# A list-scheduled two-block transformer kernel: a margin for ScalarE's and VectorE's results in the plan, scores over 128 rows, constants asked for later

## The chip, the cores and the metric

The kernel runs on one core of a Trainium2 chip. The metric is device time in microseconds of one execution; each kernel is run several times and the median is given. A profiled execution is a separate run, with its own time and its own span from the first to the last instruction.

## What is computed

Two transformer blocks follow each other on one sequence of 256 tokens of width 1024, all in fp32. The first block is a gated feed-forward layer, a mixer, and a second gated feed-forward layer. Its mixer projects to a pooling branch (four sliding means) and to attention with 8 query heads of width 64 over 2 key/value heads, a window of 128 and a learned sink per head. Cut to the part that the change touches:

```python
def swa_with_sinks(q, k, v, sinks):              # 8 query heads, 2 kv heads, G = 4, 2 blocks of 128
    s = jnp.einsum('bnqkgd,bnjkd->bnkgqj', qb, kb) * (HEAD_DIM ** -0.5)
    s = jnp.where(valid, s, NEG_INF)             # a band of 128 keys
    p = jax.nn.softmax(jnp.concatenate([s, sink], axis=-1), axis=-1)[..., :-1]
    return jnp.einsum('bnkgqj,bnjkd->bnqkgd', p, vb)
```

The second block has a mixer of its own (a state-space branch with 16 heads and a latent attention with 16 heads), attention over 256 memory tokens, and a feed-forward layer with a short convolution.

## The kernel before

Tokens stand in two tiles t = 0, 1 of 128. Every weight matrix comes from HBM once, in blocks of 128x1024 fp32. ScalarE rounds a block to fp32r (`hi`), VectorE takes the rest (`lo = raw - hi`), and TensorE forms three products, hi·hi, hi·lo and lo·hi (`mm3`, `mm2`, `projB`). So each weight block costs a cast on ScalarE, a subtraction on VectorE and 12 to 24 matmuls. Nearly all the rest (softmax, norms, convolutions, gates) runs on VectorE and ScalarE between matmuls.

**The order is planned.** `K`'s methods don't issue anything: every call records a node in `Plan` (`add`), with its estimated duration (`cost`, line 293) and its dependences. `Plan.schedule` (line 339) is a list scheduler. It keeps a clock per engine and takes, over and over, the recorded instruction that can start first by its plan; ties go to the one recorded first. An instruction is ready when the results it reads are there, and a result counts as there only a fixed time after its end, by the table `HOP` (line 206), from the producing engine to the reading one:

```python
for u in n.users:
    u.ready = max(u.ready, n.end + max(HOP[e][x] for x in u.alts))
```

The plan's times decide nothing but order: `issue` (line 501) emits the instructions in order of planned start, each engine then runs its own queue in order, and semaphores make it wait for what isn't there yet. Because all instructions are issued from one line, every row of the profile is at L514 and every tile is called `t`.

Where TensorE would have to wait in the plan, the scheduler fills in other ready matmuls, as far as buffers allow: 8 PSUM banks, a fixed number of SBUF slots of each size, and limits on how far ahead a buffer may be taken (`SLOTS`, `RESERVE`, `AHEAD`). `mixer2` is written in the order of `STEPS` (line 33), where steps of the latent attention (`mla_proj`, `mla_attn`), of the state-space branch (`ssd_x`, `ssd_z`, `ssd_rec`), of the output projection and of the memory keys take turns.

**Scores in `mixer1`** (line 1026). The query tile is transposed in pairs: column block i of `qT[t]` holds head i (of kv group 0) in partitions 0 to 63 and head 4+i (of kv group 1) in partitions 64 to 127. `kT` holds the two kv heads one over the other in the same way. A score is one fp32 matmul per head and key block, over the 64 partitions of its head, added onto a mask that bf16 matmuls put into the bank first. There are 8 of them for t = 0 and 16 for t = 1, in groups of one PSUM bank (4 or 2 heads).

**Constants.** `ffn` for the first feed-forward layer calls `side(f0)` (line 1679) from its loop over column blocks f0 = 2, 4, ..., 20; at f0 = 4, 6, 8 and 10 it asks for the constants `cst` and `cols`, builds the rotary tables and builds constants of the state-space branch. At f0 = 8 the gain `ffn1_post` is asked for (line 929). All these transfers are on the same queue (SP) as the weights, in the order that the plan gives.

Of the kernel before, what the change touches and what calls it, by code (L numbers as in the profile page):

```python
# [18 lines left out]
P = 128  # L19
# [180 lines left out]
class Node:  # L200
# [4 lines left out]

HOP = {
    "PE": {"PE": 0.0, "ACT": 200.0, "DVE": 200.0, "POOL": 240.0, "SP": 240.0},
    "ACT": {"PE": 155.0, "ACT": 140.0, "DVE": 133.0, "POOL": 180.0, "SP": 180.0},
    "DVE": {"PE": 140.0, "ACT": 118.0, "DVE": 125.0, "POOL": 166.0, "SP": 166.0},
    "POOL": {"PE": 55.0, "ACT": 33.0, "DVE": 33.0, "POOL": 40.0, "SP": 55.0},  # L210
    "SP": {"PE": 50.0, "ACT": 30.0, "DVE": 30.0, "POOL": 30.0, "SP": 0.0},
}
# [12 lines left out]
class Plan:  # L225
# [66 lines left out]
    @staticmethod  # L292
    def cost(attr, op, a, k):
        out = k.get("out", a[0] if a else None)
        size = lambda v: int(np.prod(v.shape[1:]))
        ps = any(isinstance(v, View) and v.tile.cls == "ps" for v in list(a) + list(k.values()))
        if attr == "tensor":
            if op == "transpose":
                return 109.0
            n, dt = size(out), k["rhs"].dtype  # L300
            if dt == F32R:
                return 4.0 + (0.4453 * n if n >= 256 else 4 * n / 2.4)
            return 2 * max(4 + 0.8906 * n, 109.0) if dt == F32 else 4 + 0.4453 * n
        if op == "dma_start":
            return max(int(np.prod(out.shape)) * 4 / 395.0, 300.0)
        if attr == "scalar":
            scalars = sum(isinstance(v, View) for v in (k.get("scale"), k.get("bias"), a[2] if op == "mul" else None))
            return 0.833 * size(out) + (58 if ps else 94) + 88 * scalars + (98 if "accum_out" in k else 0)
        if attr == "vector":
            if op == "reduce_max":  # L310
                return 1.04 * size(a[1]) + 70
            one = op in ("tensor_copy", "tensor_scalar") and not ps
            scalars = op in ("tensor_scalar", "scalar_tensor_tensor") and any(isinstance(v, View) for v in (a[2], a[3] if op == "tensor_scalar" else None))
            return (0.52 if one else 1.04) * size(out) + 70 + 60 * scalars
        return 550.0 if size(out) == 1 else 1.05 * size(out) + 464

    def loud(self, n):
# [299 lines left out]
class K:  # L617
# [276 lines left out]
    def ffn(self, name, src, nxt, side=None, first=None):  # L894
# [21 lines left out]
        for f0 in range(0, KF, 2) if first else (0, *range(4, KF, 2)):  # L916
# [9 lines left out]
                held = f0, [(f, evac_at[0][f], evac_at[1][f]) for f in range(2)]  # L926
                continue
            w = [self.wblocks(w_gu, KD, o + f0 * P, o + (f0 + n) * P) for o in (0, DFF)]
            if f0 == 8:
                post = self.bc(self.w1024(), a[name + "_post"][0])  # L930
            if side:
                side(f0)
# [93 lines left out]
    def mixer1(self, xT, nxt):  # L1026
        nc, a = self.nc, self.a
        self.phase = "mix"
        sink = self.rows[:, :8]
        nsink = self.const("nsink", [P, 8])  # L1030
        nc.vector.tensor_scalar(nsink, sink, -1.0, None, op0=ALU.mult)
        mask = self.const("mask", [P, 256], BF16)
        nc.vector.tensor_copy(mask, self.cst[:, C_SWA : C_SWA + 256])
# [12 lines left out]
        psc = self.bc(pw[:, 512:], a["pool_scale"][0])  # L1046
        post = self.bc(self.w1024(), a["mix_post"][0])
        kvs, us, qTs = self.w1024(), self.w1024(), self.w1024()
        u, v, kT, qT, y = [], [], [], [], []
        for t in range(2):  # L1050
            self.label(f"mix1 win t{t}")
            x, r = xT[t]
            qk = self.w1024()[:, :640]
            pk, pq = self.tps(), self.tps()
            for k in range(KD):
                self.mm3(pk[:, :256], x, k, wkv[k], k == 0, k == KD - 1)
            for k in range(KD):
                self.mm3(pq, x, k, wq[k], k == 0, k == KD - 1)
            self.label(f"mix1 qk t{t}")
            vt = kvs[:, 2 * t * P : (2 * t + 1) * P]  # L1060
            nc.vector.tensor_scalar(vt, pk[:, P:256], r, None, op0=ALU.mult)
            nc.vector.tensor_scalar(qk[:, 512:], pk[:, :P], r, 0.125, op0=ALU.mult, op1=ALU.mult)
            nc.scalar.mul(qk[:, :512].rearrange("p (i j c) -> p j i c", j=2, c=64),
                          pq.rearrange("p (j i c) -> p j i c", j=2, c=64), r)
            v.append(vt)
            self.apply_rope(qk.rearrange("p (h c) -> p h c", c=64)[:, :, :16], t, 0, 8)
            tp = self.tps()
            nc.tensor.transpose(tp[:, :P], qk[:, 512:640], self.ident)
            kt = kvs[:, (2 * t + 1) * P : (2 * t + 2) * P]
            self.copy(kt, tp[:, :P])  # L1070
            kT.append(kt)
            tp = self.tps()
            for i in range(4):
                nc.tensor.transpose(tp[:, i * P : (i + 1) * P], qk[:, i * P : (i + 1) * P], self.ident)
            qt = qTs[:, t * 512 : (t + 1) * 512]
            self.copy(qt, tp)
            qT.append(qt)

            self.label(f"mix1 u t{t}")
            pu = self.tps()  # L1080
            for k in range(KD):
                self.mm3(pu, x, k, wu[k], k == 0, k == KD - 1)
            ut = us[:, t * 512 : (t + 1) * 512]
            self.scale(ut, pu, r)
            u.append(ut)
            y.append(self.w1024())
# [4 lines left out]
        for t in range(2):  # L1091
# [8 lines left out]
            for h0 in range(0, 8, nh):  # L1100
                sc = self.tps()
                for j in range(nh):
                    nc.tensor.matmul(sc[:, j * W : (j + 1) * W], lhsT=idb, rhs=mask[:, 256 - W : 256], start=j == 0, stop=False)
                for j in range(nh):
                    g, i = (h0 + j) // 4, (h0 + j) % 4
                    for kb in range(nk):
                        o = j * W + kb * P
                        nc.tensor.matmul(sc[:, o : o + P], lhsT=qT[t][64 * g : 64 * g + 64, i * P : (i + 1) * P],
                                         rhs=kT[t - nk + 1 + kb][64 * g : 64 * g + 64, :], start=False,
                                         stop=j == nh - 1 and kb == nk - 1)  # L1110
                pT, rd = self.softmax_p(sc, nh, W, (sink[:, h0 : h0 + nh], nsink[:, h0 : h0 + nh]))
                po = self.tps()
                for j in range(nh):
                    g = (h0 + j) // 4
                    for kb in range(nk):
                        o = j * W + kb * P
                        nc.tensor.matmul(po[:, j * 64 : (j + 1) * 64], lhsT=pT[:, o : o + P],
                                         rhs=v[t - nk + 1 + kb][:, 64 * g : 64 * g + 64], start=kb == 0, stop=kb == nk - 1)
                o = 512 + 64 * h0
                nc.vector.tensor_tensor(  # L1120
                    y[t][:, o : o + 64 * nh].rearrange("p (h c) -> p h c", c=64),
                    po[:, : 64 * nh].rearrange("p (h c) -> p h c", c=64),
                    rd.unsqueeze(2).to_broadcast([P, nh, 64]), op=ALU.mult)


            self.label(f"mix1 pool t{t}")
# [538 lines left out]
def trace(k, nc, a, out):  # L1665
# [11 lines left out]
            nx.done(t)  # L1677

    def side(f0):
        if f0 == 4:  # L1680
            nc.sync.dma_start(k.cst, a["cst"])
        if f0 == 6:
            nc.sync.dma_start(k.cols, a["cols"])
            k.bc(k.rows, a["rows"][0])
        if f0 == 8:
            k.rope_tables()
        if f0 == 10:
            k.ssd_constants()

    for name, how, part in (  # L1690
# [32 lines left out]
```

## Time and profile before

| | |
|---|---|
| median of 3 runs | 983.09 us (982.91 to 983.23) |
| the profiled execution's own time | 983.15 us |
| its span, first to last instruction | 981.4 us |
| TensorE (PE) busy | 967.9 us, 6474 matmul records |
| weight loads (PEld) busy | 877.8 us |
| VectorE (DVE) busy | 704.0 us |
| ScalarE (ACT) busy | 522.6 us |
| granted TensorE clock | 0.999 over the span |

Times inside the span are counted from its first instruction. An fp32 matmul leaves two records, an fp32r or bf16 matmul and a transpose leave one. A matmul's record lasts from its start to a modelled end, and the next one starts before that end; PE is therefore shown as busy also where it issues more slowly than it could, and an idle time of PE is only what lies behind a modelled end. PEld waits are the times for which a weight load stood still, whether or not a matmul was still running beside it.

### The profile page before, as it was taken

Reading aid. Unit: us, or ns where it says so; the run is one execution under the profiler, and the core shown is the slowest. Engines: PE = TensorE matmul, PEld = TensorE weight load, DVE = VectorE, ACT = ScalarE, POOL = GpSimd, SP = SyncE. Lnnn points to the kernel's source line nnn. Section 1 sums busy time; section 2 is a strip of 40 time slices with the busy share of each in tenths; the row PEclk is TensorE's granted clock in tenths of the full one; section 3 lists DMA queues with packets and bytes.
Section 4 is the critical chain, followed back from the end, with each engine's and each line's share of the span. In section 5 each row is a group of like instructions: output and inputs, shape, how many; then the busy total and the mean of one; then the engine's idle time right before and its main releaser. Section 6 shows DMA issues by size and latency. Waiting matters only on the chain.

```text
span 981.4 us, 16455 instructions
## 1 busy us (share of the span) xinstructions
PE 967.9 (99%) x6474; PEld 877.8 (89%) x6474; DVE 704.0 (72%) x1185; ACT 522.6 (53%) x866; POOL 40.4 (4%) x53
## 2 busy tenths in 40 slices
PE   9999999999999999999999999999999999999997
PEld 8999988887889999888998988888898899999887
DVE  6985544667596556447998799997866699897543
ACT  6853424546565333245777777454555476645341
POOL 0000000310010000000200000000000010000000
PEclk9999999999999999999999999999999999999999
DMA  9985545663247555454554336045654456518411
GB/s 322 384 278 173 155 150 171 209 224 116 95 157 280 183 166 159 142 156 145 170 171 152 128 114 250 23 131 181 226 173 141 152 171 231 195 58 299 133 62 43
DMA packets 50286, 168.54 MB, mean 172 GB/s; under 512 B 5792, under 2 KB 8352, under 8 KB 50208
## 3 DMA queue, kind: packets, MB, share of 16 engines
q1 hardware_dynamic: 49920, 166.96, 51.7%
q8 instruction: 51, 0.84, 0.4%
q10 hardware_dynamic: 288, 0.52, 0.1%
q14 instruction: 27, 0.22, 0.1%
HBM read 166.42 MB, written 1.05 MB: 171 GB/s over the span
## 4 chain that ended last, share of the span: by engine, by line
PE 83%; DVE 9%; ACT 3%; DMA 2%; issue 2%; POOL 1%; SPq 0%; POOLq 0%; ACTq 0%; DVEq 0%
PE t L514 83%; DVE t L514 9%; ACT t L514 3%; DMA t<-in_ffn_w_gu_from_dram 2%; POOL t L514 1%; DMA t<-in_xT_dram 0%; ACT L514 0%; SPq L514 0%; POOLq L1719 0%; ACTq L514 0%; DVEq L514 0%; POOLq L514 0%
## 5 line engine op out<-in xcount | busy, mean ns | idle before, releaser
L514 PE MATMUL t<-t,t 128*128 128x256 f32 (+5 forms) x6466 | 964.7, 312 | 5.9 <-DVE t L514 3.4
L514 PEld LDWEIGHTS t<-t,t 128*128 128x128 f32 (+3 forms) x6450 | 875.9, 186 | 93.6 <-DVE t L514 9.4
L514 DVE TENSOR_TENSOR t<-t,t 128x1024 fp32r<-128x1024 f32 (+9 forms) x756 | 572.3, 802 | 208.3 <-PE t L514 128.1
L514 ACT CAST t<-t 128x1024 fp32r<-128x1024 f32 (+6 forms) x400 | 350.9, 908 | 224.9 <-PE t L514 190.9
L514 ACT ACTIVATE t<-t 128x512 f32<-128x512 f32 (+8 forms) x133 | 73.7, 556 | 154.4 <-DVE t L514 121.8
L514 ACT ACTIVATE t<-t,t 128x256 f32<-128x256 f32 (+5 forms) x150 | 74.3, 525 | 52.1 <-PE t L514 35.6
L514 DVE SCALAR_TENSOR_TENSOR t<-t,t,t 128x255 f32<-128x255 f32 (+5 forms) x169 | 75.3, 499 | 24.9 <-ACT t L514 21.5
L514 POOL TENSOR_TENSOR t<-t,t 128x1 f32<-128x1 f32 x38 | 36.5, 962 | 835.5 <-DVE t L514 835.4
L514 ACT COPY t<-t 128x256 f32<-128x256 f32 (+3 forms) x51 | 21.8, 446 | 18.7 <-PE t L514 18.5
L514 DVE CAST t<-t 128x512 fp32r<-128x512 f32 (+8 forms) x54 | 21.2, 395 | 7.7 <-PE t L514 4.8
L514 DVE TENSOR_REDUCE t<-t 128x1 f32<-128x125 f32 (+2 forms) x38 | 19.5, 514 | 3.5 <-PE t L514 3.5
L514 DVE SCALAR_TENSOR_TENSOR t<-t,t 128x512 f32<-128x512 f32 (+4 forms) x34 | 12.6, 378 | 10.1 <-ACT t L514 9.8
L514 DVE TENSOR_SCALAR t<-t,t 128x128 f32<-128x128 f32 (+6 forms) x31 | 9.5, 318 | 9.0 <-PE t L514 4.6
L514 ACT ACTIVATION_READ_ACCUMULATOR t<-t 128x1 f32 x61 | 11.6, 191 | 0.0
L514 ACT ACT_TABLE_LOAD x7 | 9.0, 1283 | 3.0 <-DVE t L514 2.2
L514 ACT ACTIVATION_READ_ACCUMULATOR t<-t,t 128x1 f32 x48 | 10.6, 220 | 0.0
L514 DVE TENSOR_SCALAR t<-t 128x1 f32<-128x1 f32 (+6 forms) x44 | 6.2, 166 | 4.2 <-DMA t<-in_xT_dram 2.2
L514 DVE COPY t<-t 128x512 f32<-128x512 f32 (+6 forms) x14 | 5.4, 386 | 0.6 <-PE t L514 0.6
L514 DVE SCALAR_TENSOR_TENSOR t<-t 128x1 f32<-128x1 f32 (+1 forms) x17 | 2.6, 156 | 4.3 <-ACT t L514 4.1
L514 ACT ACTIVATE t<-t,t,t 128x256 f32<-128x256 f32 x8 | 4.5, 562 | 2.1 <-DVE t L514 2.1
L514 PEld LDWEIGHTS <-t 128*128 128x128 bf16 x24 | 2.3, 114 | 3.5 <-issue 1.9
L514 POOL MEMSET t<- 128x128 f32 x5 | 1.0, 204 | 95.9 <-PE t L514 91.4
(10 smaller groups left out, 12.8 us busy)
## 6 DMA issues: line engine op xcount, KB each, us to landing
t<-in_ffn_w_gu_from_dram SPq DMA_DIRECT2D x84, 512.0 KB, 5.8
t<-in_ffn_w_down_from_dram SPq DMA_DIRECT2D x44, 512.0 KB, 3.9
t<-in_w_ffn_up_from_dram SPq DMA_DIRECT2D x44, 512.0 KB, 4.7
t<-in_w_in_from_dram SPq DMA_DIRECT2D x34, 512.0 KB, 4.8
t<-in_w_out_from_dram SPq DMA_DIRECT2D x24, 512.0 KB, 4.8
t<-in_w_ffn_down_from_dram SPq DMA_DIRECT2D x22, 512.0 KB, 5.3
t<-in_w_mem_k_from_dram SPq DMA_DIRECT2D x8, 512.0 KB, 6.7
t<-in_w_mem_q_from_dram SPq DMA_DIRECT2D x8, 512.0 KB, 4.7
```

Of the source, the lines that this page charges most:

```text
L514: getattr(getattr(nc, attr), op)(*[real(v) for v in a], **{x: real(v) for x, v in k.items()})
```

## The change

Four edits go together.

1. In the plan, a result of ScalarE or VectorE reaches TensorE 400 ns later than before (`HOP`: 155 becomes 555, 140 becomes 540), and each instruction of ScalarE and VectorE is taken as 20 ns longer. Nothing is added on the chip: no instruction waits for a time.
2. The scores of `mixer1` run over all 128 partitions. `kT` becomes a tile of 256 columns with zeros off its two diagonal blocks, so that one fp32 matmul of 256 columns gives both heads of a pair: 12 matmuls in place of 24. Heads come in the order 0, 4, 1, 5, ...; sinks are copied into that order once, `kT` takes two copies in place of one, the zeros take one memset, and the products with V are scaled in pairs of heads.
3. `side` is called for f0 = 12, 14, 16 and 18 instead of 4, 6, 8 and 10.
4. `ffn1_post` (and `ffn2_post`) is asked for at f0 = 20 instead of 8.

```diff
-    "ACT": {"PE": 155.0, "ACT": 140.0, "DVE": 133.0, "POOL": 180.0, "SP": 180.0},
-    "DVE": {"PE": 140.0, "ACT": 118.0, "DVE": 125.0, "POOL": 166.0, "SP": 166.0},
+    "ACT": {"PE": 555.0, "ACT": 140.0, "DVE": 133.0, "POOL": 180.0, "SP": 180.0},
+    "DVE": {"PE": 540.0, "ACT": 118.0, "DVE": 125.0, "POOL": 166.0, "SP": 166.0},
...
-            return 0.833 * size(out) + (58 if ps else 94) + 88 * scalars + (98 if "accum_out" in k else 0)
+            return 20 + 0.833 * size(out) + (58 if ps else 94) + 88 * scalars + (98 if "accum_out" in k else 0)
...
-            return (0.52 if one else 1.04) * size(out) + 70 + 60 * scalars
+            return (0.52 if one else 1.04) * size(out) + 90 + 60 * scalars
...
-            if f0 == 8:
+            if f0 == 20:
                 post = self.bc(self.w1024(), a[name + "_post"][0])
...
+        nc.vector.memset(kvs[:, 256:768], 0.0)
...
-            kt = kvs[:, (2 * t + 1) * P : (2 * t + 2) * P]
-            self.copy(kt, tp[:, :P])
+            kt = kvs[:, 256 * (t + 1) : 256 * (t + 2)]
+            for g in range(2):
+                self.copy(kt[64 * g : 64 * g + 64, g * P : (g + 1) * P], tp[64 * g : 64 * g + 64, :P])
...
-                for j in range(nh):
-                    g, i = (h0 + j) // 4, (h0 + j) % 4
+                for j in range(nh // 2):
+                    i = h0 // 2 + j
                     for kb in range(nk):
-                        o = j * W + kb * P
-                        nc.tensor.matmul(sc[:, o : o + P], lhsT=qT[t][64 * g : 64 * g + 64, i * P : (i + 1) * P],
-                                         rhs=kT[t - nk + 1 + kb][64 * g : 64 * g + 64, :], start=False,
-                                         stop=j == nh - 1 and kb == nk - 1)
+                        o = sc[:, 2 * j * W : 2 * (j + 1) * W].rearrange("p (g k c) -> p g k c", g=2, c=P)[:, :, kb, :]
+                        nc.tensor.matmul(o, lhsT=qT[t][:, i * P : (i + 1) * P], rhs=kT[t - nk + 1 + kb].rearrange("p (g c) -> p g c", g=2),
+                                         start=False, stop=j == nh // 2 - 1 and kb == nk - 1)
...
-        if f0 == 4:
+        if f0 == 12:
             nc.sync.dma_start(k.cst, a["cst"])
-        if f0 == 6:
+        if f0 == 14:
             nc.sync.dma_start(k.cols, a["cols"])
...
-        if f0 == 8:
+        if f0 == 16:
             k.rope_tables()
-        if f0 == 10:
+        if f0 == 18:
             k.ssd_constants()
```

**How the order moves, first place: TensorE, first scores of the second token tile in `mixer1`.** A MATMUL row names its PSUM bank, then the moving and the stationary operand. Before, t_2253 is `kT`, t_2325 is `qT`, t_629 the mask and t_185 the identity of a transpose:

```order
L514 MATMUL t_2527<-t_629,t_323 128x256
L514 MATMUL t_2527<-t_2253,t_2325 128x128 x3
L514 MATMUL t_2539<-t_185,t_2514 128x128
L514 MATMUL t_2541<-t_2123,t_2533 128x128
...
L514 MATMUL t_2527<-t_2253,t_2325 128x128
L514 MATMUL t_2562<-t_185,t_2550 128x128
```

In the changed kernel (t_259 is `kT`, t_731 the mask):

```order
L514 MATMUL t_2527<-t_731,t_319 128x256
L514 MATMUL t_2527<-t_259,t_2333 128x2x128 x2
L514 LDWEIGHTS t_319
L514 MATMUL t_2540<-t_731,t_319 128x256
L514 MATMUL t_2542<-t_2135,t_2533 128x128 x4
```

Four 64-row matmuls, the last of them between two transposes, have become two of 2x128 columns next to each other, and the transposes that read the first softmax come later.

**Second place: TensorE, `mla_attn(3)`, first head group.** Before, t_6637 takes the scores of the second token tile, t_6648 a projection that fills the time, and t_6696 the transposes of the first softmax of that step. Between the last score and the transposes 24 matmuls of 256 columns stand, of which the first and the last are shown:

```order
L514 MATMUL t_6622<-t_6327,t_6367 128x128 x4
L514 MATMUL t_6630<-t_6327,t_6435 128x256 x2
L514 MATMUL t_6637<-t_6327,t_6435 128x256 x2
L514 MATMUL t_6648<-t_4807,t_6255 128x256
...
L514 MATMUL t_6648<-t_4818,t_6373 128x256
L514 MATMUL t_6696<-t_185,t_6641 128x128 x4
```

In the changed kernel 39 of them stand there (t_6635), 15 more, and the transposes are those into t_6707:

```order
L514 MATMUL t_6611<-t_6314,t_6351 128x128 x4
L514 MATMUL t_6622<-t_6314,t_6424 128x256 x2
L514 MATMUL t_6627<-t_6314,t_6424 128x256 x2
L514 MATMUL t_6635<-t_4795,t_6234 128x256
...
L514 MATMUL t_6635<-t_4807,t_6356 128x256
L514 MATMUL t_6707<-t_178,t_6643 128x128 x4
```

**Third place: the SP queue, 27th transfer of the program.** Before, `cst` is asked for between weight blocks of the first layer:

```order
L514 DMA t_249<-in_ffn_w_gu_from_dram 128x1024
L514 DMA t_256<-in_cst_dram 128x416
L514 DMA t_265<-in_ffn_w_gu_from_dram 128x1024
L514 DMA t_289<-in_ffn_w_gu_from_dram 128x1024
L514 DMA t_307<-in_ffn_w_gu_from_dram 128x1024
L514 DMA t_329<-in_ffn_w_gu_from_dram 128x1024
L514 DMA t_337<-in_cols_dram 128x325
```

In the changed kernel the same blocks follow each other and `cst` is 43rd:

```order
L514 DMA t_246<-in_ffn_w_gu_from_dram 128x1024
L514 DMA t_262<-in_ffn_w_gu_from_dram 128x1024
L514 DMA t_285<-in_ffn_w_gu_from_dram 128x1024
...
L514 DMA t_642<-in_ffn_w_gu_from_dram 128x1024
L514 DMA t_647<-in_cst_dram 128x416
```

Sixteen weight blocks that stood behind `cst` now stand ahead of it.

## Rows read from the trace of the kernel before

**Rows 1.** The page's first part: busy time, share of the span and instructions.

```profile
PE 967.9 (99%) x6474; PEld 877.8 (89%) x6474; DVE 704.0 (72%) x1185; ACT 522.6 (53%) x866; POOL 40.4 (4%) x53
```

**Rows 2.** Stretch; busy us of PE, PEld, DVE, ACT, POOL; clock; DMA share; GB/s.

```profile
0.00:31.00 31.00, 28.22 (x208) 25.17 (x209) 20.18 (x38) 19.62 (x32) 2.09 (x11) 1.00 0.95 334
...
225.00:250.00 25.00, 25.00 (x182) 20.61 (x181) 16.22 (x50) 15.54 (x52) 1.40 (x2) 1.00 0.22 70
...
480.00:552.00 72.00, 71.09 (x483) 64.70 (x482) 63.96 (x146) 52.31 (x107) 3.00 (x4) 1.00 0.54 174
552.00:673.00 121.00, 117.70 (x788) 104.73 (x787) 115.96 (x253) 77.52 (x184) 7.84 (x12) 1.00 0.39 127
```

**Rows 3.** Waits of TensorE over the whole span: us in total, times, longest.

```profile
PEld t L514 <- DVE t L514: 9.4, 24, 0.8
...
PEld t L514 <- ACT t L514: 6.6, 20, 1.1
...
PE t L514 <- DVE t L514: 4.8, 11, 1.3
...
PE t L514 <- ACT t L514: 2.1, 4, 0.9
```

**Rows 4.** The same waits between 552 and 673 us.

```profile
PEld t L514 <- ACT t L514: 4.5, 11, 1.1
PEld t L514 <- DVE t L514: 3.4, 8, 0.7
...
PE t L514 <- ACT t L514: 1.9, 3, 0.9
...
PE t L514 <- DVE t L514: 1.2, 3, 0.5
```

**Rows 5.** TensorE's timeline around two of them: start, length, [idle before <-releaser].

```profile
606.45 11.48 PE L514 MATMUL t<-t,t 128*128 128x128 f32 x77 [0.90 <-ACT t L514]
...
672.60 2.66 PE L514 MATMUL t<-t,t 128*128 128x128 f32 x18 [0.79 <-ACT t L514]
```

**Rows 6.** TensorE by form, 120 to 170 us: busy us, mean ns of a record.

```profile
L514 PE MATMUL t<-t,t 128*128 128x512 f32 x158 | 36.8, 394 | 0.0
L514 PE MATMUL t<-t,t 128*128 128x256 f32 x114 | 13.7, 281 | 0.0
```

**Rows 7.** Waits of weight loads, 480 to 552 us, then 31 to 480 us.

```profile
PEld t L514 <- DVE t L514: 1.9, 3, 0.7
PEld t L514 <- ACT t L514: 1.0, 4, 0.4
...
PEld t L514 <- DVE t L514: 1.7, 6, 0.6
```

**Rows 8.** Short stretches of TensorE, columns as in rows 2: masks, scores, 256-column fp32.

```profile
225.97:226.09 0.11, 0.11 (x4) 0.11 (x4) 0.11 (x1) 0.07 (x1) 0.00 (x0) 1.00 0.84 256
226.09:226.24 0.15, 0.15 (x4) 0.04 (x2) 0.15 (x1) 0.13 (x1) 0.00 (x0) 1.00 1.52 165
226.24:227.32 1.09, 1.09 (x10) 0.97 (x9) 0.12 (x1) 0.56 (x1) 0.00 (x0) 1.00 0.33 102
232.38:232.80 0.42, 0.42 (x3) 0.29 (x3) 0.42 (x1) 0.40 (x3) 0.00 (x0) 1.00 0.15 59
523.11:523.54 0.43, 0.43 (x3) 0.38 (x2) 0.43 (x2) 0.00 (x0) 0.00 (x0) 1.00 0.84 224
647.93:648.65 0.72, 0.72 (x5) 0.63 (x5) 0.72 (x2) 0.00 (x0) 0.00 (x0) 1.00 0.00 0
```

**Rows 9.** Timeline, 19 to 32 us: the transfer of `cst`, and the wait at 30.51.

```profile
21.97 0.42 SPq L514 DMA_DIRECT2D t<-in_cst_dram  x1
...
27.85 1.06 ACT L514 CAST t<-t 128x1024 fp32r<-128x1024 f32 x1 [0.20 <-DMA t<-in_ffn_w_gu_from_dram]
...
30.08 0.28 DVE L514 COPY t<-t 128x128 f32<-128x128 f32 x1
...
30.51 1.31 PE L514 MATMUL t<-t,t 128*128 128x256 f32 x9 [0.82 <-DVE t L514]
```

More of the change, by code (lines that the diff above doesn't have):

```diff
@@ L1028, in mixer1 @@
         self.phase = "mix"
-        sink = self.rows[:, :8]
-        nsink = self.const("nsink", [P, 8])
+        sink, nsink = self.const("sinkp", [P, 8]), self.const("nsink", [P, 8])
+        nc.vector.tensor_copy(sink.rearrange("p (i g) -> p i g", g=2), self.rows[:, :8].rearrange("p (g i) -> p i g", g=2))
         nc.vector.tensor_scalar(nsink, sink, -1.0, None, op0=ALU.mult)
@@ L1059, in mixer1 @@
             self.label(f"mix1 qk t{t}")
-            vt = kvs[:, 2 * t * P : (2 * t + 1) * P]
+            vt = kvs[:, t * P : (t + 1) * P]
             nc.vector.tensor_scalar(vt, pk[:, P:256], r, None, op0=ALU.mult)
@@ L1113, in mixer1 @@
                 for j in range(nh):
-                    g = (h0 + j) // 4
+                    g = j % 2
                     for kb in range(nk):
@@ L1118, in mixer1 @@
                                          rhs=v[t - nk + 1 + kb][:, 64 * g : 64 * g + 64], start=kb == 0, stop=kb == nk - 1)
[L1119 to L1123, printed above, removed]
+                yo = y[t][:, 512:].rearrange("p (g i c) -> p i g c", g=2, c=64)
+                for j in range(0, nh, 2):
+                    nc.vector.tensor_tensor(
+                        yo[:, (h0 + j) // 2], po[:, j * 64 : (j + 2) * 64].rearrange("p (g c) -> p g c", c=64),
+                        rd[:, j : j + 2].unsqueeze(2).to_broadcast([P, 2, 64]), op=ALU.mult)
             self.label(f"mix1 pool t{t}")
```

## Prediction

> **What bounds the kernel now.** I read the page's busy times first. PE is busy for 967.9 of 981.4 us [rows 1], so the time is TensorE's own queue: work taken off it, or stalls taken out of it, count nearly one to one where no other engine is full. But "busy" hides stalls. A 256-column fp32r matmul comes every 0.12 us (13.7 us / 114) while its record lasts 0.281 us [rows 6], so a pause shorter than 0.16 us leaves no idle time of PE, and a longer one shows 0.16 us too little. Next I read the waits. Weight loads stood still for 9.4 us behind VectorE and 6.6 us behind ScalarE, in 44 waits; PE shows 4.8 and 2.1 us, in 15 [rows 3]. What TensorE loses to late results thus lies between 6.9 and 16.0 us. The Trainium skill ("Trainium Kernel Development and Optimization", Best Practices) calls matmul busy time a bad measure of the distance to the roofline and weight-load busy time a good one. Here the trace agrees as to the first; but weight loads are idle for 103.6 us of the span [rows 1], over six times all their waits for other engines [rows 3], so the second doesn't give the loss either.
>
> Where the waits are: between 552 and 673 us, mixer2's middle, weight loads stood 4.5 + 3.4 us in 19 waits, PE 1.9 + 1.2 us in 6 [rows 4]. With 0.16 us added for each of the 6 visible ones and half of that for each of the 13 others I get 3.1 + 1.0 + 1.0, about 5 us. From 480 to 552 us the 7 weight-load waits of 2.9 us [rows 7] make about 2 us in the same way. From 31 to 480 us it is 1.7 us behind VectorE at most [rows 7]. The third thing to read is VectorE beside this: busy for 116.0 of 121 us in 552 to 673, and for 64.0 of 72 us before that, but only for 16.2 of 25 us in mixer1's attention, where ScalarE has 15.5 [rows 2].
>
> **Scores over 128 rows.** This is work on TensorE's queue. Four 64-row scores in a row take 1.09 us, and a single one between full-height matmuls 0.42 us [rows 8]. Two masks within their row of four take 0.11 us together, the last one before the scores 0.15, so entering a run costs another 0.09 us [rows 8]. In the order of before the 24 scores stand in 14 runs: two of four, two of three (about 0.86 each) and ten single ones. That is 2.18 + 1.72 + 4.2 + 14 x 0.09 = 9.4 us. The new form, an fp32 matmul of 256 columns, isn't in the trace at 128 rows in a group, but at 98 rows, where the last of a group takes 0.43 us; and at 128 rows alone before a 512-column one, 0.72 together, less 0.23 for the latter (36.8 us / 158 [rows 6]), so 0.49 [rows 8]. Twelve cost 5.2 to 5.9 us. As they now stand mostly in pairs behind masks I take the lower value: 9.4 - 5.2 = **4.2 us** saved, 3.5 at the other end, up to 4.7 if the transposes behind a run also got slower by it.
>
> The additions (one memset of 512 columns, one copy of 8 columns, two more `kT` copies, two more scalings) are some 2 us on VectorE and ScalarE, estimated by 0.28 us for a 128-column VectorE copy [rows 9] and in proportion for the memset. Cover is the 35% of 25 us that both have free [rows 2]. Without cover the path would take the second `kT` copy alone, 0.28 us per token tile.
>
> One rule speaks against this edit: the Trainium skill ("TensorE: Matmul & The Clock Gate", Part 3) has small-K matmuls on different row groups run at once, which full-height scores give up. The rows show no such overlap: neighbours of a run use the same 64 partitions, and four take 1.09 us [rows 8]. By the rule, had pairs stood on opposite halves, the old scores would cost half and the change would lose time, by the rows 4.2 us are gained.
>
> **The margin.** It adds no instruction. It puts more TensorE work between a result's making and its use. Counting in both orders the places after 31 us where TensorE's next start came over 25 ns late behind ScalarE or VectorE, I find 46; at 42 of them more matmul time now stands between the last TensorE result that the chain needs and the waiting instruction, at one the same, at three 0.2 to 0.45 us less. In `mla_attn(3)` it is 15 matmuls, 15 x 0.12 = 1.8 us, against a wait of 0.90 + 0.16 [rows 5]. For the 0.79 us of 672.60 [rows 5], in `ssd_rec(3)`, the longer distance is some 2 us. So nearly every wait of today would be covered if results came as long after their causes as now.
>
> That "if" hangs on VectorE. Between 552 and 673 us it has 5 us free [rows 2], and its queue holds the same work after the change but for a few fillers. TensorE can't gain there more than VectorE can close of its own gaps; I take half, **2.5 us** of 5 (bounds 0 and 5). From 480 to 552 us VectorE has 8 us free, so I take **1.5 us** of 2 (0 to 2). Outside, waits are short and VectorE is idle for a third of the time: **1.0 us** (0 to 1.7). Margins can also be wasted: where there is no other work, TensorE still waits as before, and what is filled in early is missing later. What is late next is the weight blocks' subtraction on VectorE, which the filler itself needs.
>
> **Constants later.** `cst` (128 x 416 x 4 B = 0.21 MB) is asked for at 21.97 us, between weight blocks, while HBM gives 334 GB/s [rows 2, 9]: 0.64 us of transfer. Behind it the cast at 27.85 waits for its weights, then VectorE for the cast, then TensorE for VectorE until 30.51, 0.82 us visible, 0.98 with the hidden part [rows 9]. With `cst` gone the blocks come 0.64 us earlier: **0.6 us** saved, bounds 0 (if the cast was held by its queue) and 1.0. Asked for later, the constants meet no wait of TensorE: their first users are far behind. `ffn1_post` at f0 = 20 is needed only when the layer ends.
>
> **Sum.** 4.2 + 2.5 + 1.5 + 1.0 + 0.6 = 9.8 us. From the profiled execution's 983.15 us (span 981.4, with 1.8 around it, 0.06 above the median) this gives 973.3, so **973.2 us** for the median.
>
> **Rivals.** *VectorE keeps the waits.* If the stretch from 480 to 673 us is set by VectorE, whose 180 of 193 us [rows 2] must pass anyway, waits only change their place: 4.2 + 0.6 + 0.5 to 1.0 us remain, about 977.5 us. For it: VectorE at 96%; the three places with less cover lie in this stretch. Against it: PE's waits there often end on ScalarE (4.5 of 7.9 us [rows 4]), which has 36% free.
>
> *The margin starves VectorE* (slower). What TensorE does 0.4 us later by plan also reaches VectorE 0.4 us later. In 552 to 673 us 17 chains (nine softmaxes of `mla_attn(1)` to `(3)`, eight halves of `ssd_rec`) go from TensorE to VectorE about twice each, 34 hand-overs. If VectorE stood still 0.4 us at each, 13.6 us come on top of its 116, less the 5 us it has free: +8.6, less 4.8 for scores and constants, about 987 us. It decides from some 25 such hand-overs on, 25 x 0.4 - 5 = 5 us, where the other gains are used up. Against it: VectorE has several chains and weight blocks to choose from, and today hardly idles.
>
> *Full-height scores are slower.* If the old scores overlapped in pairs somewhere, they'd cost 24 x 0.27 / 2 = 3.3 us at 0.27 each (1.09 / 4 [rows 8]) against 5.2, so +1.9 in place of -4.2. With the rest of the sum this gives 979.4 us, without the margin's gain 984.4. The runs of four and the single scores [rows 8] speak plainly against it.
>
> *All waits go*: 4.7 + 5 + 2 + 1.7 + 1.0 = 14.4 us, 968.7.
>
> **How the numbers follow.** Forecast, 970 to 976 us: 0.55. VectorE keeps the waits, 976 to 979.5: 0.25. All waits go, 967.5 to 970: 0.10. VectorE starved: 0.08. Scores slower: 0.02. The range takes the first three, 967.5 to 979.5. A measurement of this kernel can tell 0.2%, 2.0 us. Faster by more than that (below 981.1) are the first three, but for 0.02 of the second in which new waits take the rest, and half of the last: 0.89. Within: those 0.02, a quarter of the starved case and half of the last, 0.05. Slower: 0.06.
>
> **What would show it.** Scores: no records of 64 rows, 24 records of 256 columns in mixer1, that stretch of 25 us with some 4 us less for the same work. Margin: weight-load waits between 480 and 673 us below half of 10.8 us, VectorE's share there at 97% or more. Constants: the wait at 30.51 below 0.4 us. I am wrong if the waits in 480 to 673 us add up to as much as before, if VectorE waits for PE there for more than some 5 us, or if a new wait appears in the feed-forward layers, which have none now.

## The result, and the profile after

The changed kernel takes 973.71 us (median of 4 runs, 970.78 to 975.53) against 983.16 us (4 runs, 982.91 to 983.64). The ratio is 0.9899, with a 95% interval of 0.9878 to 0.9921: 9.45 us faster, where 9.9 were forecast. Its runs spread over 4.8 us, those of before over 0.7. That spread has a cause, which the experiments find. The profiled execution took 973.88 us, with a span of 972.1 us and a mean granted clock of 0.996 (before 0.999).

The page's busy times after the change (engine, busy us, share of the span, records), to be read against [rows 1]: 24 records of PE are gone, VectorE has the same busy time, and POOL has 7.8 us more for the same instructions (40.4 before). POOL's 7.8 us turn out to be the trace of what holds the gain back.

```profile
PE 958.4 (99%) x6450; PEld 878.5 (90%) x6450; DVE 704.0 (72%) x1185; ACT 518.4 (53%) x867; POOL 48.2 (5%) x53
```

The scores: matmuls by form in 224.5 to 249 us (form, count, busy us, mean ns). The 64-row form is gone. The 24 records are the 12 new scores.

```profile
L514 PE MATMUL t<-t,t 128*128 128x256 f32 x24 | 6.6, 384 | 0.0
```

The waits between 480 and 673 us (us in total, times, longest us), against 10.8 us of weight-load waits before [rows 4, 7]: VectorE's part is nearly gone (5.3 us in 11 waits before, 1.3 now). ScalarE's has not become smaller (5.6 us in 15 waits before). It now stands in half as many, longer waits, and PE's own behind ScalarE grew from 2.1 to 3.9 us. PE's visible idle time in this window, behind both engines, thus went up from 4.0 to 4.9 us.

```profile
PEld t L514 <- ACT t L514: 5.9, 7, 1.9
PE t L514 <- ACT t L514: 3.9, 3, 1.8
PEld t L514 <- DVE t L514: 1.3, 3, 0.7
PE t L514 <- DVE t L514: 1.0, 2, 0.6
```

Where PE's three waits behind ScalarE stand, in PE's timeline (start, length, first form of the piece, in brackets the idle time before it and what ended it). All three are in `ssd_rec`; the third, at 661.26, is shown below. A fourth, of 0.23 us between two matmuls at 634.55, is too short to show as idle time.

```profile
622.60 22.04 PE L514 MATMUL t<-t,t 128*128 128x128 f32 x133 [1.62 <-ACT t L514]
645.16 14.34 PE L514 MATMUL t<-t,t 128*128 128x128 f32 x90 [0.52 <-ACT t L514]
```

VectorE did not fill up: 111.64 us of 121 in the second stretch, where it had 116.0 [rows 2]. Behind the wait at 622.60 the granted clock fell to 0.70 and 0.87, that is, TensorE ran at 1.2 GHz, half its speed, for 0.6 x 4 + 0.26 x 4 = 3.4 us. The windows of the changed kernel (stretch, its length, busy us of PE, PEld, DVE, ACT, POOL with records, clock, DMA share, GB/s):

```profile
225.00:250.00 25.00, 25.00 (x183) 22.87 (x182) 18.60 (x58) 16.30 (x56) 2.34 (x5) 1.00 0.29 101
552.00:673.00 121.00, 116.30 (x762) 104.89 (x761) 111.64 (x238) 73.70 (x166) 14.47 (x12) 0.99 0.41 136
622.00:626.00 4.00, 3.40 (x16) 3.10 (x17) 1.91 (x5) 1.73 (x5) 0.01 (x1) 0.70 0.02 4
626.00:630.00 4.00, 4.00 (x30) 3.78 (x30) 3.52 (x8) 1.98 (x6) 0.55 (x1) 0.87 0.16 20
```

Where the 9.3 us of the span come from, stage by stage. I took the start of the same matmul in both traces; the lead is before's time less the changed kernel's.

| place | lead, us |
|---|---|
| first score of `mixer1` | 1.4 |
| last `w_out` product of `mixer1` | 6.5 |
| start of the second feed-forward layer's down projection | 7.2 |
| first `ssd_rec` | 12.8 |
| third `ssd_rec` | 7.1 |
| end of `mixer2` | 8.7 |
| end | 9.3 |

So the scores and the covers of `mixer1` gave 5.1 us, the covers of `mixer2`'s first half some 5, and from the first `ssd_rec` to the end of `mixer2` 4.1 us of the lead were lost again. (The 7.1 between them overstates the loss. The scores aside, 10 records fewer than before stand ahead of the first `ssd_rec`, and 9 more ahead of the third.) The question is what that loss is.

**What ScalarE waited for there.** The waiting chain is a norm's: VectorE makes the mean of squares, POOL raises it to the power -1/2 (one element per partition), ScalarE scales by it, and TensorE transposes the scaled tile. The timeline of the changed kernel at the last of the four waits:

```profile
657.05 0.15 DVE L514 TENSOR_SCALAR t<-t 128x1 f32<-128x1 f32 x1
657.11 0.27 DVE L514 TENSOR_REDUCE t<-t 128x1 f32<-128x125 f32 x1
...
657.28 3.38 POOL L514 TENSOR_TENSOR t<-t,t 128x1 f32<-128x1 f32 x1 [6.37 <-DVE t L514]
657.30 2.95 DVE L514 TENSOR_TENSOR t<-t,t 128x512 f32<-128x512 f32 x3
...
660.70 0.51 ACT L514 ACTIVATE t<-t,t 128x256 f32<-128x256 f32 x1 [2.86 <-POOL t L514]
...
661.26 0.44 PE L514 MATMUL t<-t,t 128*128 128x128 f32 x2 [1.76 <-ACT t L514]
```

The power took 3.38 us. Others of the same form take 0.55 (the changed kernel's POOL timeline, two powers apart by what VectorE did beside them):

```profile
619.08 2.93 POOL L514 TENSOR_TENSOR t<-t,t 128x1 f32<-128x1 f32 x1 [4.42 <-DVE t L514]
626.92 0.55 POOL L514 TENSOR_TENSOR t<-t,t 128x1 f32<-128x1 f32 x1 [4.91 <-DVE t L514]
```

The one at 657.28 begins 0.02 us before VectorE's `TENSOR_TENSOR` with two SBUF inputs and ends 0.41 us after the third of these, which run back to back. Before the change it was there too. The 0.79 us of [rows 5] at 672.60 come behind such a power, at 670.36 (timeline of before):

```profile
667.07 0.55 POOL L514 TENSOR_TENSOR t<-t,t 128x1 f32<-128x1 f32 x1 [8.78 <-DVE t L514]
...
670.36 1.65 POOL L514 TENSOR_TENSOR t<-t,t 128x1 f32<-128x1 f32 x1 [2.73 <-DVE t L514]
670.38 1.22 DVE L514 TENSOR_TENSOR t<-t,t 128x1024 fp32r<-128x1024 f32 x1
```

The Trainium skill ("SBUF — State Buffer", SBUF: two separate sides) says that a VectorE operation with two SBUF inputs and a GpSimd operation that reads SBUF share a port pair under an exclusive lock, which the one that starts first keeps for its whole instruction. The trace agrees as to the lock (0.55 against 1.65 to 3.38 us). As to who gets it, POOL's record starts 0.02 us earlier at 657.28 and at 670.36, and POOL is still the one that is held.

The kernel knows of this: its plan has a shield. After the operation whose result a power reads, `Plan` puts a `filler` on VectorE, a `reduce_max` over 125 columns of a spare tile (the `TENSOR_REDUCE` at 657.11), so that no operation with two SBUF inputs starts as POOL does. At 657 us the filler's record ends at 657.38, 0.10 us after the power's start, but VectorE's next operation already starts at 657.30. At the powers behind the other three waits (619.08, 632.49 and 642.97) no filler stands at all. There the plan has the operation with two SBUF inputs start 314 ns after the one whose result the power reads, just behind the 300 ns that it keeps clear; with the costs of before it would be 274 ns. On the chip it starts 0.26 us after, 0.03 us ahead of the power. By these sums it is the 20 ns of edit 1 that took the shield away at these three, and over the whole kernel the fillers went from 16 to 11 (VectorE's groups by form, before and after):

```profile
L514 DVE TENSOR_REDUCE t<-t 128x1 f32<-128x125 f32 x16 | 4.4, 276 | 0.0
L514 DVE TENSOR_REDUCE t<-t 128x1 f32<-128x125 f32 x11 | 3.0, 275 | 0.0
```

The margin without the 20 ns was not run. Over the whole kernel 12 powers before and 14 after took more than 0.7 us, in all 15.6 and 21.4 us above their 0.55. Most are harmless, since TensorE doesn't wait for them; four in `ssd_rec` aren't.

My theory was then: the margin covers what the forecast said it would, and what remains late is the held power. The rival was the forecast's own: VectorE's supply sets `mixer2`'s middle, and the waits are where its lack comes out.

### The profile page after: what moved, and what is told of

The parts are those of the page before. It is cut to its first block, busy times and chain, and to the rows that moved or that the text cites. A ratio compares the mean times of both kernels' runs of the same rounds, so it can differ in the third digit from the quotient of the medians.

```text
span 972.1 us, 16396 instructions
## 1 busy us (share of the span) xinstructions
PE 958.4 (99%) x6450; PEld 878.5 (90%) x6450; DVE 704.0 (72%) x1185; ACT 518.4 (53%) x867; POOL 48.2 (5%) x53
## 4 chain that ended last, share of the span: by engine, by line
PE 87%; DVE 7%; issue 2%; POOL 1%; ACT 1%; DMA 1%; SPq 0%; POOLq 0%; DVEq 0%; ACTq 0%
PE t L514 87%; DVE t L514 7%; POOL t L514 1%; ACT t L514 1%; DMA t<-in_ffn_w_gu_from_dram 1%; DMA t<-in_xT_dram 0%; SPq L514 0%; ACT L514 0%; POOLq L1722 0%; POOLq L514 0%; DVEq L514 0%; ACTq L514 0%
## 5 line engine op out<-in xcount | busy, mean ns | idle before, releaser
L514 PE MATMUL t<-t,t 128*128 128x256 f32 (+6 forms) x6442 | 954.8, 312 | 6.2 <-ACT t L514 4.2
L514 PEld LDWEIGHTS t<-t,t 128*128 128x128 f32 x6426 | 876.5, 187 | 83.5 <-ACT t L514 6.9
L514 ACT ACTIVATE t<-t 128x512 f32<-128x512 f32 (+9 forms) x133 | 73.7, 559 | 166.6 <-DVE t L514 126.0
L514 ACT ACTIVATE t<-t,t 128x256 f32<-128x256 f32 (+6 forms) x149 | 73.0, 522 | 56.3 <-PE t L514 31.7
L514 POOL TENSOR_TENSOR t<-t,t 128x1 f32<-128x1 f32 x38 | 42.2, 1113 | 802.5 <-DVE t L514 789.7
L514 ACT COPY t<-t 128x256 f32<-128x256 f32 (+4 forms) x54 | 22.6, 441 | 17.1 <-PE t L514 16.8
L514 DVE CAST t<-t 128x512 fp32r<-128x512 f32 (+9 forms) x55 | 21.8, 399 | 13.4 <-PE t L514 4.7
L514 DVE TENSOR_REDUCE t<-t 128x2 f32<-128x512 f32 (+2 forms) x33 | 17.6, 547 | 0.7 <-PE t L514 0.7
L514 POOL COPY t<-t 128x8 f32<-128x8 f32 (+1 forms) x6 | 4.9, 843 | 25.8 <-DMA t<-in_cst_dram 25.6
```

Of the source, the lines that this page charges most:

```text
L514: getattr(getattr(nc, attr), op)(*[real(v) for v in a], **{x: real(v) for x, v in k.items()})
```

## The experiments

First three kernels with one part of the change each, and one that keeps the changed kernel and makes the shield longer. All four ran beside the same runs of before (median 982.9 us, 24 runs).

**The margin alone.**

```diff
-    "ACT": {"PE": 155.0, ...
-    "DVE": {"PE": 140.0, ...
+    "ACT": {"PE": 555.0, ...
+    "DVE": {"PE": 540.0, ...
```

(and the 20 ns of the two costs)

> The kernel before with the plan's margin alone (HOP +400 ns and 20 ns more per ScalarE and VectorE instruction); scores and constants as before. Theory A (the prediction's term for the margin): 5.0 us saved, 978.2 us. Theory B (read off the two traces by stage: 9.3 us in all, of which 1.0 is gained by the start of mixer1 and 5.1 in mixer1's attention up to the last w_out product): 3.3 us or less for the margin, about 980 us. In either case waits of weight loads over the span fall from 16 to about 10 us and what remains stands in a few long waits of ssd_rec.

980.98 us (12 runs, 977.41 to 982.97), ratio 0.998 (0.9969 to 0.999): only 1.9 us, far from theory A's 5.0 and within theory B's "3.3 us or less". The waits of VectorE fall as in the changed kernel, and ScalarE's stay, behind held powers (POOL's timeline and the waits over the whole span of this kernel):

```profile
624.04 2.94 POOL L514 TENSOR_TENSOR t<-t,t 128x1 f32<-128x1 f32 x1 [4.41 <-DVE t L514]
...
662.29 3.39 POOL L514 TENSOR_TENSOR t<-t,t 128x1 f32<-128x1 f32 x1 [6.36 <-DVE t L514]
```

```profile
PEld t L514 <- ACT t L514: 6.0, 7, 1.9
...
PEld t L514 <- DVE t L514: 3.4, 8, 0.9
```

Here the clock fell behind two of the waits, not one (windows, columns as above; the clock is the third number from the end):

```profile
627.00:631.00 4.00, 3.43 (x18) 3.10 (x18) 2.12 (x6) 2.02 (x6) 0.00 (x0) 0.74 0.00 0
666.00:670.00 4.00, 3.73 (x18) 3.63 (x19) 2.77 (x6) 2.40 (x4) 0.00 (x0) 0.57 0.66 241
```

That fits the spread: a stretch at half clock comes in some executions and not in others. The changed kernel's quickest run, 970.78 us, has a mean clock of 0.999, its other three 0.996 to 0.997. The 12 runs of the margin alone follow their clock too: 977.41 us at 0.998, 982.64 at 0.991, where the runs of before have 0.998 or 0.999. In its one run at nearly full clock the margin alone is thus 5.5 us faster than the median of before. The clock makes up most of the 3.6 us between that run and the median: their mean clocks differ by some 0.0035, which is 3.4 of 979 us by estimate. Only for the profiled run is it shown where the half clock stands.

**The scores alone.**

```diff
-                        nc.tensor.matmul(sc[:, o : o + P], lhsT=qT[t][64 * g : 64 * g + 64, i * P : (i + 1) * P],
+                        nc.tensor.matmul(o, lhsT=qT[t][:, i * P : (i + 1) * P], rhs=kT[t - nk + 1 + kb].rearrange("p (g c) -> p g c", g=2),
```

(with the zeros, the two copies and the order of heads that go with it)

> The kernel before with the scores over 128 rows alone; plan and constants as before. Theory A (the prediction): 4.2 us saved, 979.0 us, 24 records of 256 columns at 128 rows in place of 48 of 64 rows. Theory B (stage table): up to 5.1 us, 978.1. Rival: without a margin the transposes and the products with V behind shorter scores wait for the softmax, and 2 us or less are left, 981 us or more.

980.39 us (6 runs, 979.73 to 980.72), ratio 0.9972 (0.9961 to 0.9983): 2.5 us, between the two theories and the rival. In the profiled run, from the first score to the last `w_out` product, the stage takes 44.82 us, for 48.65 in before: 3.8 of the forecast 4.2 us are there. Without the margin TensorE stands still in `mixer1` for more than in before, which had 1.2 us of weight-load waits behind VectorE and 0.4 behind ScalarE in this window; the changed kernel has none. The waits of the scores' kernel, 200 to 290 us:

```profile
PEld t L514 <- DVE t L514: 1.8, 4, 0.6
...
PEld t L514 <- ACT t L514: 1.1, 4, 0.4
PE t L514 <- DVE t L514: 0.7, 3, 0.3
```

**The constants alone.**

```diff
-        if f0 == 4:
+        if f0 == 12:
             nc.sync.dma_start(k.cst, a["cst"])
```

(and the other four places of edits 3 and 4)

> The kernel before with the later constants alone (side at f0 = 12 to 18, ffn1_post at 20). Theory: 0.6 to 1.0 us saved, 982.2 to 982.6 us, the wait at 30.5 us of 0.82 us halved. Rival: the block's cast was held by its own queue, no change, 983.2 us.

982.65 us (11 runs, 981.28 to 983.77), ratio 0.9997 (0.9988 to 1.0005): nothing that can be measured, as the rival had it. The wait stayed (PE's timeline of this kernel): 0.86 us, where it was 0.82 [rows 9].

```profile
30.64 1.54 PE L514 MATMUL t<-t,t 128*128 128x256 f32 x11 [0.86 <-DVE t L514]
```

ScalarE's cast after the one at 27.85, of a block that landed beside `cst`, did come 0.63 us earlier (29.89 to 29.26). TensorE wasn't waiting for it: it waits behind three subtractions on VectorE, which follow each other and stand where they stood. The two timelines at that cast and that run, first before, then with the later constants:

```profile
29.89 1.05 ACT L514 CAST t<-t 128x1024 fp32r<-128x1024 f32 x1 [0.99 <-DMA t<-in_ffn_w_gu_from_dram]
26.37 3.80 DVE L514 TENSOR_TENSOR t<-t,t 128x1024 fp32r<-128x1024 f32 x3 [0.15 <-ACT t L514]
...
29.26 1.05 ACT L514 CAST t<-t 128x1024 fp32r<-128x1024 f32 x1 [0.23 <-DMA t<-in_ffn_w_gu_from_dram]
26.50 3.79 DVE L514 TENSOR_TENSOR t<-t,t 128x1024 fp32r<-128x1024 f32 x3 [0.16 <-ACT t L514]
```

**The changed kernel with a longer shield.** The filler takes up to 250 columns and is planned with 330 ns in place of 200, and the time that the plan keeps clear of operations with two SBUF inputs lasts 230 ns in place of 100, that is up to 430 ns after the start of the operation whose result the power reads. It also shifts the order somewhat, as any change of the plan does.

```diff
-        cols = min(P, max(8, int((ns - 70) / 1.04)))
+        cols = min(2 * P, max(8, int((ns - 70) / 1.04)))
...
-                    out.append(self.filler(max(T[e], quiet[1] - 200.0), 200.0))
+                    out.append(self.filler(max(T[e], quiet[1] - 330.0), 330.0))
...
-                    quiet = st + 200.0, st + 300.0
+                    quiet = st + 200.0, st + 430.0
...
-        nc.spare = self.const("quiet", [P, P])
+        nc.spare = self.const("quiet", [P, 2 * P])
```

> The changed kernel with the filler on VectorE that shields a GpSimd power made longer (330 ns planned in place of 200, the shielded time 230 ns in place of 100). Theory C: the waits left in ssd_rec (0.2 to 1.9 us, 4.6 us in all, ended by a ScalarE scaling that waited for GpSimd) come from GpSimd's 1-element power, which takes 0.55 us alone and 1.5 to 3.4 us when a VectorE instruction with two SBUF inputs starts within 0.1 us of it, and after a wait of 1.8 us TensorE runs at half clock for 3.4 us. With the longer shield nearly all powers take 0.55 us, and 3 to 5 us are saved: 969 to 971 us, runs closer together, clock 0.999. Theory D: VectorE is full in this stretch and the waits only move: 973 to 974 us, with the powers short all the same.

966.89 us (4 runs, 966.85 to 967.34), ratio 0.9837 (0.9824 to 0.985). This beats both kernels, by 6.8 us the changed one, more than theory C had (969 to 971), and the spread is gone. Its timeline at a power shows the longer filler, and VectorE's first operation with two SBUF inputs 0.29 us after the power's start:

```profile
618.39 0.14 DVE L514 TENSOR_SCALAR t<-t 128x1 f32<-128x1 f32 x1
618.46 0.28 DVE L514 TENSOR_TENSOR t<-t,t 128x128 f32<-128x128 f32 x1
618.65 0.40 DVE L514 TENSOR_REDUCE t<-t 128x1 f32<-128x250 f32 x1
618.68 0.55 POOL L514 TENSOR_TENSOR t<-t,t 128x1 f32<-128x1 f32 x1 [4.84 <-DVE t L514]
618.97 0.68 DVE L514 TENSOR_TENSOR t<-t,t 128x512 f32<-128x512 f32 x1
```

Its fillers number 16 again. Only 2 of its powers take over 0.7 us, 1.8 us in excess. POOL's busy time on its page is 20 us below that of the changed kernel:

```profile
PE 955.7 (99%) x6450; PEld 877.1 (91%) x6450; DVE 704.9 (73%) x1190; ACT 518.4 (54%) x867; POOL 27.9 (3%) x53
```

The waits between 480 and 673 us are all but gone:

```profile
PEld t L514 <- DVE t L514: 1.2, 5, 0.4
PEld t L514 <- ACT t L514: 1.1, 3, 0.4
...
PE t L514 <- ACT t L514: 0.2, 1, 0.2
PE t L514 <- DVE t L514: 0.2, 1, 0.2
```

And two windows answer the rival: in `mixer2`'s middle PE is busy for 119.4 of 120 us with VectorE at 96%, and from 480 to 673 us for 192.4 of 193 with VectorE at 95%.

```profile
535.00:655.00 120.00, 119.40 (x806) 109.25 (x805) 115.44 (x258) 79.27 (x190) 5.35 (x11) 1.00 0.37 131
480.00:673.00 193.00, 192.39 (x1286) 175.73 (x1285) 182.82 (x398) 129.63 (x288) 7.28 (x14) 1.00 0.45 152
```

The size fits the cause. In the changed kernel the four waits in `ssd_rec`, with the prediction's 0.16 us added to the three that show as idle time, are 1.78, 0.23, 0.68 and 1.92 us, 4.6 in all, and 3.4 us at half the clock cost up to 1.7: together 6.3 of 6.8 us. The rest can be the shifted order.

The second four ran beside runs of before with a median of 983.25 us (13 runs), 0.35 us above that of the first four. Where times from the two sets are compared below, the figure behind "or" allows for this.

**Before with the longer shield** (the same diff on the kernel before). It asks whether the shield is worth this without the margin.

> The kernel before with the longer shield alone, no margin. Theory: most of its waits are short ones behind VectorE results that no power delays, so only the two waits behind slow powers go (0.95 us at 672.6, 0.25 us at 793.7): 981.5 to 982 us. Rival: slow powers also set much of what looked like a lack of margin, 979 us or less.

980.33 us (10 runs, 979.89 to 981.07), ratio 0.9973 (0.9963 to 0.9982): 2.9 us, between the theory and its rival. The waits between 480 and 673 us stay nearly as they were, 5.3 us behind VectorE and 4.4 behind ScalarE for weight loads. Without cover, results are late for other reasons. The waits that did go there, 1.2 us of weight loads, are less than half of the 2.9 us. About 1 us of it stands ahead of `mixer1` in the profiled run, where the wait at 30.51 is down to 0.16 us though its constants are asked for as before.

**The margin and the longer shield**, without the scores and the constants.

> The kernel before with the margin and the longer shield; scores and constants as before. Theory: the margin alone was worth 1.9 us only because the powers were locked out; with them free it takes out nearly all the 10 us of waits behind 31 us, and the scores' 4 to 5 us are what separates this from 966.9: 971 to 973 us. Rival: margin and shorter scores need each other, 975 us or more.

971.97 us (4 runs, 971.12 to 975.98), ratio 0.9896 (0.9874 to 0.9917). The four kernels make a table:

| | shield as before | longer shield |
|---|---|---|
| no margin | 983.2 | 980.3 |
| margin | 981.0 | 972.0 |

The margin gives 1.9 us alone, the shield 2.9 alone, both together 11.3. Each gain is taken against before of its own set. Each edit removes one of two things of which either keeps TensorE waiting, and part of what the margin lacks alone is time at half clock. From here to the changed kernel with the longer shield, scores and constants give 971.97 - 966.89 = 5.1 us, or 4.7.

The profiled execution was the longest of this kernel's, 975.98 us. Its windows show TensorE at half clock (0.50) for a whole stretch of `mixer1`'s attention, with no idle time of PE there:

```profile
228.00:239.00 11.00, 11.00 (x60) 7.78 (x59) 6.67 (x23) 7.12 (x30) 0.55 (x1) 0.82 0.42 164
239.00:245.00 6.00, 6.00 (x26) 5.00 (x26) 2.21 (x8) 2.66 (x9) 0.00 (x0) 0.50 0.01 3
```

That is 0.36 x 11 + 6 = 10 us at 1.2 GHz in work with the old 64-row scores, transposes and short products. What set it off wasn't tried.

**Half and double the margin**, on the changed kernel with the longer shield. The first kernel has 200 ns:

```diff
-    "ACT": {"PE": 555.0, ...
-    "DVE": {"PE": 540.0, ...
+    "ACT": {"PE": 355.0, ...
+    "DVE": {"PE": 340.0, ...
```

> The changed kernel with the longer shield and half the margin (HOP 355 and 340). If most waits were under 0.25 us of lag in the plan, 967 to 968 us, no difference that can be told from 966.9; if the plan lags by up to 0.4 us, 968.5 to 971.

969.83 us (4 runs, 968.75 to 971.06), 2.9 us above the 400 ns kernel, or 2.6: the second of the two cases. Weight loads wait for VectorE again (waits over its whole span):

```profile
PEld t L514 <- DVE t L514: 6.3, 14, 1.0
...
PE t L514 <- DVE t L514: 4.5, 10, 1.5
```

The second has 955 and 940, a margin of 800 ns, which is where the starvation rival should show:

> The changed kernel with the longer shield and double the margin (HOP 955 and 940). Theory: what is left to cover is 1 to 2 us, so 965.5 to 967.5. Rival of the prediction (VectorE starved by work that TensorE does later): 970 us or more, with VectorE's waits for PE between 540 and 670 us at 10 us or more.

968.26 us (4 runs, 967.42 to 969.0), 1.4 us above the 400 ns kernel, or 1.0, which is barely clear of the noise. It lies between the theory and the rival. VectorE does not starve. It waits for PE for 2.9 us between 540 and 670 us, as with 400 ns (2.8). The new waits are TensorE's behind ScalarE (2.8 us against 1.1):

```profile
DVE t L514 <- PE t L514: 2.9, 3, 2.4
PEld t L514 <- ACT t L514: 2.8, 5, 0.9
...
PEld t L514 <- DVE t L514: 1.7, 4, 0.6
```

## Why the prediction was right, and where it wasn't

The time, the sign and the likeliest case came true: 973.7 against 973.2 us. That the sum fits is partly luck: the margin's waits went out and others came in, and the step for the constants was wrong. By its steps:

**Scores: mechanism and size right.** The 12 new scores come every 0.43 to 0.49 us in the trace, 5.3 us in all, for a forecast of 5.2. As forecast, no 64-row records are left and 24 of 256 columns stand there, and the stage of `mixer1` from the first score to the last `w_out` product went from 48.65 to 43.54 us with all edits, to 44.82 with the scores alone and to 48.00 with the margin alone. So the scores are worth 3.8 us of that stage without the margin and 4.5 with it, both within the forecast's 3.5 to 4.7. Alone the edit keeps less in the stage because TensorE, being done sooner, then stands still for results. Over the whole kernel it gave 2.5 us alone; where the rest of the 3.8 went is not shown. On top of the margin, with the powers free, scores and constants gave 4.7 to 5.1. The forecast costed the edits as if each kept its worth alone; it does not. The additions found their cover: in 225 to 250 us VectorE is busy for 18.6 us (16.2 before [rows 2]) and ScalarE for 16.3 (15.5), and PE has no idle time. The rival of full-height scores that cost more falls.

**Margin: the direction right, one step wrong.** The step that failed is "TensorE can't gain there more than VectorE can close of its own gaps". With 400 ns of margin and free powers, TensorE is busy for 192.39 of the 193 us from 480 to 673 and VectorE for 182.82, so 95%, for 188.79 and 179.92 in before. I had read VectorE's high share as a bound. It was none: the waits of weight loads there went from 10.9 to 2.3 us, while VectorE closed less than 3 of its 13 idle us. The margin was worth 8.4 us (980.33 to 971.97), not 5.0, where the powers were free. What held the gain back in the changed kernel was a step that the forecast didn't have: the power on POOL, which the 0.55 us of most powers and POOL's 4% share made look free. "But for a few fillers" missed it too: there were five fewer, four of them by edit 1 alone (12 left). Of the signs I named, neither came: weight-load waits went from 10.8 to 7.2 us, not below half, and VectorE's share went down, to 92%. Of the signs of being wrong one did come, just: VectorE's waits for PE in 480 to 673 us rose from 2.4 to 5.2 us, where I had said "more than some 5 us" (3.5 with the longer shield). These were the signs of the wrong step, and they told so in the profile although the total was right. "What is late next" was the place to ask. I named the weight blocks' subtraction on VectorE. It was ScalarE's scaling behind POOL, and the row for it was there: the 0.79 us at 672.60 [rows 5], whose chain has a power of 1.65 us in it.

So 5.0 was near the right size for the wrong reason: 9.45 - 5.1 leaves 4.4 us for all else in the full change. Alone the margin gave 1.9. Held powers don't tell the two apart: PE's waits behind them are 1.64, 0.57 and 1.74 us with the margin alone and 1.62, 0.52 and 1.76 in the full change. Two other things do. The clock is lower with the margin alone (0.991 to 0.998, for 0.996 to 0.999). And 1.4 of the 4.4 us are the lead at the first score of `mixer1`, of which about 1 us also shows in the profiled run of before with the longer shield, which has none of the four edits.

**Constants: the step was wrong, within its bounds.** "With `cst` gone the blocks come 0.64 us earlier" did happen, by 0.63 us (29.89 to 29.26). The step that failed is "Behind it the cast at 27.85 waits for its weights": that cast stands at 27.98 with the later constants, so `cst` didn't hold it. The one that `cst` held is the next, at 29.89, and TensorE starts at 30.51, before that cast is done. Alone the edit changed nothing that could be measured, and the wait was 0.86 us. In the changed kernel it was 0.34, so my sign, below 0.4, appeared, but it is no sign of the edit. The wait is 0.16 us in before with the longer shield, where `cst` is asked for early, and 0.65 in the changed kernel with the longer shield, where it is late.

**Rivals.** "VectorE keeps the waits" falls with the longer shield: the waits went, with VectorE at 95%, where it had 93 in before. "The margin starves VectorE" falls with the 800 ns kernel, whose new waits stand behind ScalarE. "All waits go", 968.7 us, was not what this change did, but it was possible: the longer shield brought 966.9.

## What to carry to other kernels

When two things keep an engine waiting at the same place, taking away either shows little; test them in pairs before calling one worthless (here 1.9 and 2.9 us apart, 11.3 together). After adding slack, follow each wait that is left back to its first late instruction, and compare the length of that instruction with others of its own form: a small operation that takes 3.4 us in place of 0.55 is held by something. A change of the plan's costs can also undo a protection that the plan gives: count its instructions before and after (here 16 and 11 fillers). A high busy share of the engine that feeds the critical one is no bound until its own waits are gone.

## What the runs showed of the hardware

- A GpSimd power on one element per partition takes 0.55 us alone and up to 3.39 us in these rows (8.54 at 189.38 us in before) when a VectorE operation with two SBUF inputs starts with it. It is then held not for that operation only but until a back-to-back run of them ends. In the traces this befell nearly all powers that began up to about 0.04 us before such an operation's start, or while one ran (1.27 us at 477.14 in the changed kernel); an exception is 266.30 there, 0.55 us with the operation 0.02 us later. Where the operation started 0.1 us later or more, as with 0.29 us above, the power took 0.55 to 0.6. A VectorE cast with one SBUF input held a power too: 0.85 us at 696.96 in before.
- A VectorE operation's record can begin 0.08 us before the previous one's ends (657.30 and 657.38), so a filler protects for less time than its record lasts. At 657.28 this is what made the 125-column shield too short; at the other three waits the filler was missing.
- Single waits of TensorE of 1.6 to 1.8 us were followed by up to 3.4 us at half clock in some executions. The 1.76 us at 661.26 in the changed kernel was not (clock 1.00 from 655 to 668 us). Half clock makes such a wait cost up to twice its length, and makes the time of the kernel spread. Half clock also came without any visible wait, in one execution, for some 10 us of 64-row and short matmuls; its cause stays open.
